# Hybrid decoder layer: negated attention scores, mLSTM keys scaled on ScalarE, one product of the gate spread on VectorE, and bias copies placed later in the program

## The chip, the cores and the metric

One NeuronCore of a Trainium2 chip runs the whole layer in one launch. The engines are TensorE (PE, with its weight loads PEld), VectorE (DVE), ScalarE (ACT), GpSimd (POOL) and SyncE (SP, which issues most transfers). The metric is the device time of one execution in microseconds (us), the median of several runs.

## The reference, cut to what matters

A layer maps x (1024 tokens, 1024 channels) to x of the same shape. It normalises x, projects it, runs an mLSTM (4 heads of 128) and a windowed attention (8 heads of 64) side by side, projects their outputs back, and then retrieves experts.

```python
h = rms_norm(x, norm1_g); proj = h @ w_in
# mLSTM: chunks of 128, with a state carried from chunk to chunk
c = silu(causal_short_conv(u, conv_w, conv_b))
qm = c @ wq_m;  km = (c @ wk_m) * 128 ** -0.5
c_chunk = einsum('bhnl,bhnlk,bhnlv->bhnkv', exp(g - m_loc), km, vm)
# attention: scores with a position bias, softmax by the running maximum
s = einsum(q, k) * 64 ** -0.5 + bias
p = exp(s - max(s)); o = p @ v / sum(p)
x = x + concat(ym, ya) @ w_out
# PEER: 8 heads, top 16 of 128 x 128 experts, per token 128 experts
idx, gate = top_k(...), softmax(...)
a = gelu(x_norm . expert_u[idx]) * gate
x = x + a @ expert_v[idx]
```

## The kernel before

The tokens are eight tiles of 128. They go through the first part in three groups: group 0 is tiles 0 and 1, group 1 is tiles 2 to 5, group 2 is tiles 6 and 7. For each group `channels_in`, `project_gates`, `project_conv`, `project_values` and `project_attention` multiply by the input weights, which `halves` loads in blocks (`wr`) and splits into a rounded part on ACT (`wh`, L168) and a remainder on DVE (`wl`, L170). `attention` and `mlstm` follow, woven together, then `queries`: the output projection (`acco`), the second norm (its GpSimd power is `r2o`), the query projection (`accq`) and the top-16 search on DVE.

The experts are done in two ways. The 512 tokens of group 1 go through all 16,384 experts on PE (`dense_experts`, tiles `pu` and `pv`, 6,144 matmuls of 512 columns), with a matrix of gates that is zero where an expert wasn't chosen. `spread_gates` builds that matrix: for four tokens at a time DVE makes one-hot rows (`hot`, L724), ACT copies one side (`e1`, L728), the other side is multiplied by the gate (`e2`), PE multiplies the two (`pg`, L739) and ACT copies the result out (`gs`, L740). Of the 128 steps of four tokens, every second one has `e2` made by ACT in four instructions (L732), the others by one GpSimd product (L734). In the trace both `e1` and `e2` are called `e`.

The other 512 tokens (tiles 0, 1, 6, 7) are sparse: GpSimd gathers one expert row for 128 tokens at a time by an indirect transfer (`gt`, L803, five buffers). `experts_in` multiplies a gathered row by the token on DVE (L815, `idx`); `experts_out_pe` of tiles 0 and 1 sums the gathered rows by PE (`pov`, L846, with weights `wv` by DVE, `idxt`), `experts_out` of tiles 6 and 7 by DVE (L860). These gathers run beside everything else from the second norm of group 0 on.

The position bias of the attention is made at the start: `rel_d` holds a row of 1152 numbers for each head, and eight transfers copy each row 128 times to `skew_d[h]` in DRAM (L134, 576 KB each), from which `attention_operands` later reads shifted windows (`bt`).

In `scores`, PE makes up to 512 scores at a time (`sc`, L511), DVE adds the bias and keeps the running maximum in one instruction (L513), a small DVE instruction negates the maximum (L516), and ACT takes the exponential with it as bias (L517). In `mlstm`, the keys `pk` are scaled by a factor for each token and by 128 ** -0.5 on DVE (`kt`, L428) and enter the state's update (`pcc`, `cst`). Once a head, GpSimd takes a power there (`sm`, L465).

The program is written in the order of the last lines, but the order in which each engine runs it is set when it is built: `TileContext(nc, schedule_with_timeline_sim=True)` lays the instructions out by a simulated timeline, so an edit anywhere can move instructions elsewhere. Each engine then runs its own list in order, and waits at an instruction whose inputs or buffers aren't ready.

Of the kernel before, what the change touches and what calls it, by code (L numbers as in the profile page):

```python
# [11 lines left out]
F32 = mybir.dt.float32  # L12
# [4 lines left out]
AF = mybir.ActivationFunctionType  # L17
ALU = mybir.AluOpType
# [25 lines left out]
def hybrid_layer(ctx, tc, x, g1, w_in, w_if, conv_w, conv_b, wq, wk, if_b, mh_g, skip, qn_g, kn_g,  # L44
# [84 lines left out]
        nc.sync.dma_start(rel_d, rv)  # L129

    skew_d = {}
    for h in range(AH):
        skew_d[h] = dram.tile([P, RL], F32, name=f"skew{h}")
        nc.sync.dma_start(skew_d[h], rel_d[h:h + 1].to_broadcast([P, RL]))  # L134


    halo = consts.tile([P, MH, 3], F32, name="halo")
# [216 lines left out]
    def gates(g, cl, ml, gi, gf):  # L354

        tile0, n = GROUPS[g]
        full = [MH, n, P]
        mr = cl.tile(full, F32, name="mr", bufs=2)
        ab = ml.tile([MH, n * P], F32, name="ab", tag="w2r", bufs=2)
        nc.vector.scalar_tensor_tensor(ab, gf, -1.0, gf, op0=ALU.mult, op1=ALU.max)  # L360
        nc.scalar.activation(ab, ab, AF.Exp, scale=-1.0)
        nc.scalar.activation(ab, ab, AF.Ln, bias=1.0)
        nc.vector.scalar_tensor_tensor(gf, gf, 0.0, ab, op0=ALU.min, op1=ALU.subtract)
        bc = ml.tile(full, F32, name="bc")
        for c in range(n):
            f = gf[:, c * P:(c + 1) * P]
            nc.vector.tensor_tensor_scan(bc[:, c], f, f, 0.0, op0=ALU.add, op1=ALU.bypass)
        nc.vector.tensor_tensor(gi, gi, bc, op=ALU.subtract)

        top = ml.tile([MH, n], F32, name="top")  # L370
        nc.vector.tensor_reduce(top, gi, AX.X, ALU.max)
        nc.vector.tensor_tensor_scan(mst[:, tile0 + 1:tile0 + n + 1], top, bc[:, :, P - 1],
                                     mst[:, tile0:tile0 + 1], op0=ALU.max, op1=ALU.add)
        for c in range(n):
            t = tile0 + c
            nc.vector.tensor_tensor_scan(mr[:, c], gi[:, c], gi[:, c], mst[:, t:t + 1], op0=ALU.max, op1=ALU.max)
        pc = pst.tile([P, 4, n, MH], F32, name="pc", tag="tp")
        for q in range(4):
            row = gi
            if q:  # L380
                row = ml.tile(full, F32, name="row", tag="w2r", bufs=2)
            if q == 1:
                nc.vector.tensor_tensor(row, mst[:, tile0:tile0 + n, None].to_broadcast(full), mr,
                                        op=ALU.subtract)
            elif q == 2:
                nc.vector.scalar_tensor_tensor(row, bc, -1.0, mr, op0=ALU.mult, op1=ALU.subtract)
            elif q == 3:
                nc.vector.tensor_tensor(row, gi, mr[:, :, P - 1:P].to_broadcast(full), op=ALU.subtract)
            for c in range(n):
                nc.tensor.transpose(pc[:, q, c], row[:, c], ident[0:MH, 0:MH])  # L390
        wcol = cl.tile([P, n, MH], F32, name="wcol", bufs=2)
        nc.vector.tensor_copy(wcol, pc[:, 0])
        ecol = cl.tile([P, 3, n, MH], F32, name="ecol", bufs=2)
        nc.scalar.activation(ecol, pc[:, 1:4], AF.Exp)
        pa = pst.tile([P, n, MH], F32, name="pa", tag="tp")
        nc.tensor.matmul(pa, lastsel, ecol[:, 0], start=True, stop=True)
        acol = cl.tile([P, n, MH], F32, name="acol", bufs=2)
        nc.vector.tensor_copy(acol, pa)
        return mr, wcol, ecol, acol

    def mlstm(g, half, h, ml, cols, mix):
# [23 lines left out]
            nc.tensor.matmul(pk[:, c], cT[:, c * P:(c + 1) * P], wqk[:, 1], start=True, stop=True)  # L425
        kt = ml.tile([P, HT, P], F32, name="kt", tag="w2m", bufs=5 if g == 0 else 6)
        for c in range(HT):
            nc.vector.tensor_scalar(kt[:, c], pk[:, c], ecol[:, 2, c, h:h + 1], P ** -0.5,  # L428
                                    op0=ALU.mult, op1=ALU.mult)
        pd = pml.tile([P, HT, P], F32, name="pd", tag="ml")  # L430
        nc.tensor.matmul(pd, negsel[:, h], mr, start=True, stop=False)
        nc.tensor.matmul(pd, ident, mask[:, None, :].to_broadcast([P, HT, P]), start=False, stop=True)
# [67 lines left out]
    def scores(g, at, op, hp, i):  # L500
        kp, vp, qp, bts, po, den = op
        hs = slice(hp * AD, (hp + 1) * AD)
        NP = (GROUPS[g][0] + GROUPS[g][1]) * P
        W = (GROUPS[g][0] + i + 1) * P
        mx = at.tile([P, 4], F32, name="mx", bufs=4)
        ss = at.tile([P, NP], F32, name="ss", bufs=2)
        m = LOW
        for u0 in range(0, W, 512):
            u1 = min(W, u0 + 512)
            sc = psc.tile([P, 512], F32, name="sc")  # L510
            nc.tensor.matmul(sc[:, :u1 - u0], qp[hs, i * P:(i + 1) * P], kp[hs, u0:u1], start=True, stop=True)  # L511
            j = 1 if u1 == W else 0
            nc.vector.tensor_tensor_reduce(ss[:, u0:u1], sc[:, :u1 - u0], bts[hp][:, NP - W + u0:NP - W + u1],  # L513
                                           1.0, m, ALU.add, ALU.max, mx[:, j:j + 1])
            m = mx[:, j:j + 1]
        nc.vector.tensor_scalar(mx[:, 2:3], mx[:, 1:2], -1.0, None, op0=ALU.mult)  # L516
        nc.scalar.activation(ss[:, :W], ss[:, :W], AF.Exp, bias=mx[:, 2:3], accum_out=den[:, hp, i:i + 1])  # L517
        return ss

    def values(g, at, op, hp, i, ss):  # L520
# [191 lines left out]
    def spread_gates(t, gb, psg):  # L712

        half = TQ
        for b in range(P // TB):
            gs = gb.tile([P, P, TB], F32, name="gs", bufs=2)
            for q in range(TB // half):
                c0 = b * TB + q * half
                ids, gate = ROWS[t]
                full = [P, P, half]  # L720
                hot = []
                for side in range(2):
                    o = gb.tile(full, BF16, name="hot", bufs=6)
                    nc.vector.tensor_tensor(o, ids[:, side, None, c0:c0 + half].to_broadcast(full),  # L724
                                            key128, op=ALU.is_equal)
                    hot.append(o.rearrange("p e t -> p t e"))
                e1 = gb.tile([P, half, P], F32, name="e1", bufs=3)
                nc.scalar.copy(e1, hot[0])  # L728
                e2 = gb.tile([P, half, P], F32, name="e2", bufs=3)
                if q % 2:  # L730
                    for j in range(half):
                        nc.scalar.activation(e2[:, j], hot[1][:, j], AF.Copy, scale=gate[:, c0 + j:c0 + j + 1])  # L732
                else:
                    nc.gpsimd.tensor_tensor(e2, hot[1], gate[:, c0:c0 + half, None].to_broadcast([P, half, P]),  # L734
                                            op=ALU.mult)
                for j0 in range(0, half, 4):
                    pg = psg.tile([P, 4, P], F32, name="pg")
                    for j in range(4):
                        nc.tensor.matmul(pg[:, j], e1[:, j0 + j], e2[:, j0 + j], start=True, stop=True)  # L739
                    nc.scalar.copy(gs[:, :, q * half + j0:q * half + j0 + 4].rearrange("p e t -> p t e"), pg)  # L740
# [139 lines left out]
    cols = project_gates(0, cm.tiles, *hx)  # L880
    project_conv(0, *hx)
    project_values(0, *hx)
    project_attention(0, *hx)
    mx = Scope("mx", "right")
    mix = zq.tiles.tile([P, KD, GROUPS[0][1] * P], F32, name="mix0", tag="z")
# [144 lines left out]
```

## Time and profile before

| what | value |
|---|---|
| runs | 3044.32 us median of 3 (3024.34 to 3048.78) |
| profiled execution | 3025.4 us, its span 3023.6 us |
| mean granted TensorE clock | 0.943 |
| busy share of the span | PE 90%, DVE 78%, POOL 47%, ACT 41% |

The span is the time from the first to the last instruction of one profiled execution. A share of busy time is a mean over stages with different limits: the dense experts fill PE for the second half of the span, while the first half changes its limit several times. The granted clock is that of TensorE, 1.0 for 2.4 GHz and 0.5 for 1.2 GHz.

### The profile page before, as it was taken

What the parts mean: (1) busy time and instruction counts of PE and PEld (TensorE: products, weight loads), DVE (VectorE), ACT (ScalarE), POOL (GpSimd) and SP (SyncE); (2) the same over time, 40 slices, a digit from 0 to 9 for tenths busy, and PEclk for the clock granted to TensorE, in tenths of its full rate; (3) what the DMA queues carried; (4) which work ended last, traced back from release to release, by engine and by line L of the source; (5) the groups of instructions that cost most, each with busy time, mean ns of one, the idle gap of its engine ahead of it and who ended that gap; (6) DMA issues with size and microseconds to landing.
All of it is one profiled execution on the core that took longest, in us unless ns stands there. A gap on an engine that the chain in (4) does not pass through costs nothing.

```text
span 3023.6 us, 42958 instructions
## 1 busy us (share of the span) xinstructions
PE 2735.5 (90%) x14382; PEld 2157.6 (71%) x14382; DVE 2350.9 (78%) x5552; ACT 1231.9 (41%) x2279; POOL 1414.7 (47%) x1139
## 2 busy tenths in 40 slices
PE   6977776898879998888899999999999999999999
PEld 5867665676656664667666787787887877788877
DVE  4559987788976887769854788888888888898873
ACT  4643332364424224899962232233322232232222
POOL 0100567546644445545543555555555555555530
PEclk9979888797889998899999999999999999999999
DMA  6644799898988987898888999999999999999982
GB/s 194 192 153 127 260 322 345 281 326 302 329 310 316 316 306 251 312 327 307 296 299 299 321 332 321 323 333 318 336 331 325 332 324 326 333 335 331 340 287 74
DMA packets 370898, 891.51 MB, mean 295 GB/s; under 512 B 34119, under 2 KB 135495, under 8 KB 366580
## 3 DMA queue, kind: packets, MB, share of 16 engines
q0 software_dynamic: 147456, 536.94, 50.0%
q1 hardware_dynamic: 209076, 307.78, 31.0%
q10 hardware_dynamic: 14144, 44.05, 3.8%
q8 instruction: 113, 1.85, 0.2%
q14 instruction: 109, 0.89, 0.1%
HBM read 831.97 MB, written 61.38 MB: 295 GB/s over the span
## 4 chain that ended last, share of the span: by engine, by line
PE 48%; DMA 13%; issue 13%; DVE 12%; POOL 7%; ACT 6%; SPq 1%; POOLq 0%; DVEq 0%; ACTq 0%
POOL gt L803 7%; DMA gg<-gate_d 5%; PE pu L155 5%; PE pu L154 4%; PE pu L153 4%; PE pv L154 4%; PE pv L153 4%; PE pv L155 4%; PE accq L192 4%; PE pov L846 3%; PE acco L192 3%; DMA gt<-in_expert_u_dram,idx 2%; DVE gt L815 2%; DMA wr<-in_w_in_dram 2%; DMA gt<-in_expert_v_dram,idxt 2%
## 5 line engine op out<-in xcount | busy, mean ns | idle before, releaser
L803 POOL DMA_INDIRECT gt<-in_expert_u_dram,idx x512 | 665.2, 1299 | 630.9 <-DVE gt L815 400.1
L815 DVE SCALAR_TENSOR_TENSOR gt<-gt,h2s 128x1024 f32<-128x1024 f32 x512 | 617.6, 1219 | 71.3 <-DMA gt<-in_expert_u_dram,idx 69.5
L803 POOL DMA_INDIRECT gt<-in_expert_v_dram,idx x256 | 342.5, 1338 | 299.6 <-DVE acc L860 258.5
L154 PE MATMUL pv<-vlo,dah 128*128 128x512 f32 x1024 | 404.1, 395 | 15.1 <-DVE vlo L792 15.0
L803 POOL DMA_INDIRECT gt<-in_expert_v_dram,idxt x256 | 273.3, 1068 | 308.1 <-PE pov L846 250.7
L153 PE MATMUL pu<-h2th,uhi 128*128 128x512 f32 x1024 | 407.3, 398 | 2.2 <-ACT da L765 1.2
L155 PE MATMUL pu<-h2th,ulo 128*128 128x512 f32 x1024 | 407.1, 398 | 1.3 <-DVE ulo L760 1.3
L154 PE MATMUL pu<-h2tl,uhi 128*128 128x512 f32 x1024 | 406.8, 397 | 0.0
L155 PE MATMUL pv<-vhi,dal 128*128 128x512 f32 x1024 | 402.1, 393 | 0.0
L790 ACT CAST vhi<-vr 128x512 fp32r<-128x512 f32 x256 | 158.1, 621 | 457.3 <-PE pv L155 443.8
L860 DVE SCALAR_TENSOR_TENSOR acc<-gt,act,acc 128x1024 f32<-128x1024 f32 x256 | 327.8, 1280 | 10.9 <-DMA gt<-in_expert_v_dram,idx 8.5
L153 PE MATMUL pv<-vhi,dah 128*128 128x512 f32 x1024 | 324.1, 395 | 9.8 <-ACT vhi L790 9.8
L168 ACT CAST wh<-wr 128x512 fp32r<-128x512 f32 x291 | 179.2, 620 | 260.4 <-DMA wr<-in_w_in_dram 55.2
L170 DVE TENSOR_TENSOR wl<-wr,wh 128x512 fp32r<-128x512 f32 x291 | 199.7, 688 | 59.2 <-ACT wh L168 57.3
L792 DVE TENSOR_TENSOR vlo<-vr,vhi 128x512 fp32r<-128x512 f32 x256 | 175.3, 686 | 85.9 <-ACT vhi L790 85.8
L758 ACT CAST uhi<-ur 128x1024 fp32r<-128x1024 f32 x128 | 134.5, 1051 | 262.2 <-PE pu L154 261.8
L154 PEld LDWEIGHTS pv<-vlo,dah 128*128 128x128 f32 x1024 | 193.9, 189 | 64.4 <-DVE vlo L792 20.6
L153 PEld LDWEIGHTS pv<-vhi,dah 128*128 128x128 f32 x1024 | 192.6, 189 | 60.9 <-ACT vhi L790 14.3
L155 PEld LDWEIGHTS pu<-h2th,ulo 128*128 128x128 f32 x1024 | 193.6, 189 | 50.9 <-issue 3.4
L153 PEld LDWEIGHTS pu<-h2th,uhi 128*128 128x128 f32 x1024 | 193.5, 189 | 49.0 <-ACT uhi L758 1.9
L154 PEld LDWEIGHTS pu<-h2tl,uhi 128*128 128x128 f32 x1024 | 193.5, 189 | 47.5 <-issue 1.7
L155 PEld LDWEIGHTS pv<-vhi,dal 128*128 128x128 f32 x1024 | 194.3, 190 | 43.1 <-issue 0.8
(278 smaller groups left out, 5681.9 us busy)
## 6 DMA issues: line engine op xcount, KB each, us to landing
ur<-in_expert_ut_dram SPq DMA_DIRECT2D x128, 512.0 KB, 6.2
vr<-in_expert_v_dram SPq DMA_DIRECT2D x256, 256.0 KB, 5.9
wr<-in_w_in_dram SPq DMA_DIRECT2D x144, 256.0 KB, 5.7
gate_d<-gs ACTq DMA_DIRECT2D x32, 1024.0 KB, 6.6
gg<-gate_d SPq DMA_DIRECT2D x16, 2048.0 KB, 19.4
wr<-in_w_query_dram SPq DMA_DIRECT2D x96, 256.0 KB, 3.9
wr<-in_w_out_dram SPq DMA_DIRECT2D x48, 256.0 KB, 5.0
gt<-in_expert_u_dram,idx POOLq DMA_INDIRECT x512, 7.1
```

What stands on the lines that cost most here:

```text
L153: nc.tensor.matmul(ps, lh, rh, start=first, stop=False)
L154: nc.tensor.matmul(ps, lh, rl, start=False, stop=False)
L155: nc.tensor.matmul(ps, ll, rh, start=False, stop=last)
L168: nc.scalar.copy(wh, wr)
L170: nc.vector.tensor_tensor(wl, wr, wh.bitcast(F32), op=ALU.subtract)
L192: nc.tensor.matmul(o, l, r, start=k == 0 and c == 0 and j == 0, stop=k == KD - 1 and j == 2, skip_group_check=True)
L758: nc.scalar.copy(uh, ur)
L790: nc.scalar.copy(vh, vr)
L792: nc.vector.tensor_tensor(vl, vr, vh.bitcast(F32), op=ALU.subtract)
L803: nc.gpsimd.indirect_dma_start(out=gt, out_offset=None, in_=table, in_offset=bass.IndirectOffsetOnAxis(ap=idx[:, j:j + 1], axis=0))
L815: nc.vector.scalar_tensor_tensor(gt, gt, 1.0, h2, op0=ALU.mult, op1=ALU.mult, accum_out=pr[:, j:j + 1])
L860: nc.vector.scalar_tensor_tensor(acc, gt, COEF[t][:, j:j + 1], acc, op0=ALU.mult, op1=ALU.add)
```

## The change

Four edits. The scores are kept negated: the one DVE instruction now forms -(score + bias) and a running minimum, and the exponential takes its input times -1, so that the small negation L516 goes. The keys' second factor 128 ** -0.5 is multiplied once into a column of `ecol` for each group, and the scaling of the keys becomes an ACT instruction. The GpSimd product of the spread becomes the same product on DVE. And the code that issues the bias copies stands behind the first `project_values`.

```diff
-    for h in range(AH):
-        skew_d[h] = dram.tile([P, RL], F32, name=f"skew{h}")
-        nc.sync.dma_start(skew_d[h], rel_d[h:h + 1].to_broadcast([P, RL]))
+    def skew(heads):
+        for h in heads:
+            skew_d[h] = dram.tile([P, RL], F32, name=f"skew{h}")
+            nc.sync.dma_start(skew_d[h], rel_d[h:h + 1].to_broadcast([P, RL]))
...
+        nc.vector.tensor_scalar(ecol[:, 2], ecol[:, 2], P ** -0.5, None, op0=ALU.mult)
...
-            nc.vector.tensor_scalar(kt[:, c], pk[:, c], ecol[:, 2, c, h:h + 1], P ** -0.5,
-                                    op0=ALU.mult, op1=ALU.mult)
+            nc.scalar.activation(kt[:, c], pk[:, c], AF.Copy, scale=ecol[:, 2, c, h:h + 1])
...
-        m = LOW
+        m = -LOW
...
-                                           1.0, m, ALU.add, ALU.max, mx[:, j:j + 1])
+                                           -1.0, m, ALU.add, ALU.min, mx[:, j:j + 1])
...
-        nc.vector.tensor_scalar(mx[:, 2:3], mx[:, 1:2], -1.0, None, op0=ALU.mult)
-        nc.scalar.activation(ss[:, :W], ss[:, :W], AF.Exp, bias=mx[:, 2:3], accum_out=den[:, hp, i:i + 1])
+        nc.scalar.activation(ss[:, :W], ss[:, :W], AF.Exp, scale=-1.0, bias=mx[:, 1:2],
+                             accum_out=den[:, hp, i:i + 1])
...
-                    nc.gpsimd.tensor_tensor(e2, hot[1], gate[:, c0:c0 + half, None].to_broadcast([P, half, P]),
+                    nc.vector.tensor_tensor(e2, hot[1], gate[:, c0:c0 + half, None].to_broadcast([P, half, P]),
...
     project_values(0, *hx)
+    skew(range(AH))
     project_attention(0, *hx)
```

By count, DVE loses 64 negations and 32 key scalings and gains 64 products and 3 small scalings; ACT gains 32 key scalings; POOL loses 64 products; PE and SP keep the number of their instructions.

**The bias copies.** SP's list at the start of the program, before (`wr` are weight blocks, `skew` the copies):

```order
L166 DMA wr<-in_w_in_dram 128x512
L129 DMA rel_d<-rv 8x1152
L166 DMA wr<-in_w_in_dram 128x512
L134 DMA skew_145<-rel_d 128x1152
L134 DMA skew_147<-rel_d 128x1152
L134 DMA skew_149<-rel_d 128x1152
L134 DMA skew_151<-rel_d 128x1152
L134 DMA skew_153<-rel_d 128x1152
L134 DMA skew_155<-rel_d 128x1152
L134 DMA skew_157<-rel_d 128x1152
L134 DMA skew_159<-rel_d 128x1152
L166 DMA wr<-in_w_in_dram 128x512
```

and now, up to the first read of a bias:

```order
L129 DMA rel_d<-rv 8x1152
L168 DMA wr<-in_w_in_dram 128x512
L136 DMA skew_824<-rel_d 128x1152
L168 DMA wr<-in_w_in_dram 128x512
L136 DMA skew_826<-rel_d 128x1152
L136 DMA skew_828<-rel_d 128x1152
L136 DMA skew_830<-rel_d 128x1152
L136 DMA skew_832<-rel_d 128x1152
L136 DMA skew_834<-rel_d 128x1152
L136 DMA skew_836<-rel_d 128x1152
L136 DMA skew_838<-rel_d 128x1152
L495 DMA bt<-skew_824 128x256
```

One weight block has moved from behind the eighth copy to behind the first; the copies themselves stay where they were, and the rows that follow (three reads of a bias, ten weight blocks) are the same in both.

**The gathers.** POOL's list at the end of group 1's attention, up to the norm behind its output projection (`sm` is the power of one mLSTM head, `r2o` that of the norm, `rqo` those of group 2's attention projections), before:

```order
L161 TENSOR_TENSOR rqo<-rq,mhalf 128x8
L803 DMA gt<-in_expert_u_dram,idx 128x1024 x7
L161 TENSOR_TENSOR rqo<-rq,mhalf 128x8
L465 TENSOR_TENSOR sm<-sm,mhalf 128x2
L803 DMA gt<-in_expert_u_dram,idx 128x1024 x7
L161 TENSOR_TENSOR rqo<-rq,mhalf 128x8
L803 DMA gt<-in_expert_u_dram,idx 128x1024 x11
L465 TENSOR_TENSOR sm<-sm,mhalf 128x2
L803 DMA gt<-in_expert_u_dram,idx 128x1024 x14
L465 TENSOR_TENSOR sm<-sm,mhalf 128x2
L803 DMA gt<-in_expert_u_dram,idx 128x1024 x29
L161 TENSOR_TENSOR r2o<-r_8378,mhalf 128x4
```

and now:

```order
L467 TENSOR_TENSOR sm<-sm,mhalf 128x2
L806 DMA gt<-in_expert_u_dram,idx 128x1024 x4
L163 TENSOR_TENSOR rqo<-rq,mhalf 128x8
L806 DMA gt<-in_expert_u_dram,idx 128x1024 x12
L467 TENSOR_TENSOR sm<-sm,mhalf 128x2
L806 DMA gt<-in_expert_u_dram,idx 128x1024 x10
L467 TENSOR_TENSOR sm<-sm,mhalf 128x2
L806 DMA gt<-in_expert_u_dram,idx 128x1024 x31
L163 TENSOR_TENSOR r2o<-r_8333,mhalf 128x4
L806 DMA gt<-in_expert_u_dram,idx 128x1024 x2
L467 TENSOR_TENSOR sm<-sm,mhalf 128x2
L806 DMA gt<-in_expert_u_dram,idx 128x1024 x7
```

Before, all 256 gathers of `experts_in` for tiles 0 and 1 stood ahead of `r2o`; now 9 of them stand behind it. Counted over POOL's whole list from group 1's first `sm` to `r2o`, 145 gathers stood there before and 130 now, and 111 and 117 stood ahead of that first `sm`. On PE, 16 more of the 512 `pov` matmuls stand behind the last `pg` (84 for 68).

**The spread.** DVE's list in the first half of `spread_gates` (`x` is the output projection's sum of group 2), before:

```order
L724 TENSOR_TENSOR hot<-ids,key_107 128x512 x8
L838 SCALAR_TENSOR_TENSOR wv<-iota_103,aT 128x64
L724 TENSOR_TENSOR hot<-ids,key_107 128x512 x4
L838 SCALAR_TENSOR_TENSOR wv<-iota_103,aT 128x64
L724 TENSOR_TENSOR hot<-ids,key_107 128x512
L569 TENSOR_TENSOR x_13012<-x_13012,acco 128x256 x2
L724 TENSOR_TENSOR hot<-ids,key_107 128x512
L569 TENSOR_TENSOR x_13014<-x_13014,acco 128x256
```

and now:

```order
L727 TENSOR_TENSOR hot<-ids,key_107 128x512 x2
L572 TENSOR_TENSOR x_12951<-x_12951,acco 128x256 x2
L572 TENSOR_TENSOR x_12953<-x_12953,acco 128x256 x2
L737 TENSOR_TENSOR e_11231<-hot,grow 128x512
L727 TENSOR_TENSOR hot<-ids,key_107 128x512 x4
L172 TENSOR_TENSOR wl<-wr,wh 128x512
L841 SCALAR_TENSOR_TENSOR wv<-iota_103,aT 128x64
L727 TENSOR_TENSOR hot<-ids,key_107 128x512 x2
L737 TENSOR_TENSOR e_11264<-hot,grow 128x512
```

The products stand between the one-hot rows, one for every four of them, and whatever stands behind a product on DVE waits with it. Of the 64, 26 stand ahead of the first top-16 search of group 2, 37 between it and the last `hot`, and one behind that.

## Rows read from the trace of the kernel before

**Rows 1.** Windows by stage: busy us (instructions), granted clock, DMA share, GB/s.

```profile
core 0: us, PE busy (x) PEld busy (x) DVE busy (x) ACT busy (x) POOL busy (x), PEclk, DMA share, GB/s
535.00:922.00 387.00, 331.71 (x1932) 263.10 (x1930) 318.39 (x752) 173.56 (x396) 217.73 (x170) 0.85 0.89 311
922.00:1203.00 281.00, 269.02 (x1501) 160.58 (x1501) 218.10 (x1200) 95.93 (x181) 131.72 (x129) 0.95 0.85 295
1203.00:1360.00 157.00, 129.39 (x933) 98.00 (x929) 107.94 (x270) 138.59 (x285) 88.68 (x80) 0.90 0.89 315
1360.00:1541.00 181.00, 155.84 (x1141) 122.76 (x1142) 165.76 (x636) 170.03 (x328) 91.96 (x84) 0.96 0.84 297
1600.00:3010.00 1410.00, 1384.99 (x5983) 1110.91 (x5982) 1131.63 (x1517) 407.01 (x612) 705.87 (x533) 0.99 0.90 313
```

**Rows 2.** Chain of waits, shares by line, 535 to 922 us.

```profile
by line: PE acco L192 12.2%; DVE gt L815 12.1%; DMA gt<-in_expert_u_dram,idx 9.9%; issue 9.6%; DMA wr<-in_w_in_dram 6.9%; PE sc L511 6.2%; PE po L532 4.6%; DVE wl L170 3.0%; POOL gt L803 2.9%; PE pp L528 2.5%; DMA wr<-in_w_out_dram 2.1%; DM
```

**Rows 3.** Timeline of the start: start us, us, engine, line, what.

```profile
18.86 5.57 SPq L134 DMA_DIRECT2D skew<-rel_d  x8
...
24.53 0.59 SPq L166 DMA_DIRECT2D wr<-in_w_in_dram  x1
...
32.57 23.64 SPq L166 DMA_DIRECT2D wr<-in_w_in_dram  x10
...
39.44 0.62 ACT L168 CAST wh<-wr 128x512 fp32r<-128x512 f32 x1 [5.97 <-DMA wr<-in_w_in_dram]
...
40.11 0.58 PE L192 MATMUL accu<-hth,wh 128*128 128x256 f32 x1 [4.75 <-ACT wh L168]
...
42.01 1.12 ACT L168 CAST wh<-wr 128x512 fp32r<-128x512 f32 x2
```

**Rows 4.** Lines L516, L428 and L448: count, ns min/median/max, first and last start.

```profile
L516 DVE TENSOR_SCALAR mx<-mx x64: 134/146/155, 133.1 to 1185.0; 128x1 f32<-128x1 f32 x64
...
L428 DVE TENSOR_SCALAR kt<-pk,ecol x32: 329/342/351, 67.9 to 1150.7; 128x128 f32<-128x128 f32 x32
...
L448 ACT ACTIVATE it<-pn,ecol x32: 349/370/376, 80.3 to 1180.2; 128x129 f32<-128x129 f32 x32
```

**Rows 5.** Tile gt, 535 to 922 us.

```profile
L815 DVE SCALAR_TENSOR_TENSOR gt<-gt,h2s x157: 1173/1217/1280, 534.4 to 921.3; 128x1024 f32<-128x1024 f32 x157
L815 DVE DVE_READ_ACCUMULATOR gt<-gt,h2s x156: 70/81/86, 535.5 to 914.0; 128x1 f32 x156
```

**Rows 6.** Waits, 1150 to 1600 us: total us, times, longest.

```profile
POOL e L734 <- PE pg L739: 35.8, 10, 9.9
...
ACT gs L740 <- PE pg L739: 21.9, 16, 5.1
...
DVE hot L724 <- POOL e L734: 16.1, 8, 3.2
```

**Rows 7.** Tile hot, 1203 to 1558 us, and groups by line, 1190 to 1560 us.

```profile
L724 DVE TENSOR_TENSOR hot<-ids,key x255: 368/414/1946, 1202.7 to 1541.8; 128x512 bf16<-128x512 bf16 x128
...
L734 POOL TENSOR_TENSOR e<-hot,grow x64: 1039/1058/1893, 1209.2 to 1544.5; 128x512 f32<-128x512 bf16 x64
...
L724 DVE TENSOR_TENSOR hot<-ids,key 128x512 bf16<-128x512 bf16 x256 | 125.5, 509 | 51.0 <-ACT e L728 26.4 <-POOL e L734 16.1 <-ACT e L732 7.2
```

**Rows 8.** The page's group of `wl`: busy us, mean ns, idle before.

```profile
L170 DVE TENSOR_TENSOR wl<-wr,wh 128x512 fp32r<-128x512 f32 x291 | 199.7, 688 | 59.2 <-ACT wh L168 57.3
```

**Rows 9.** Timeline in the spread: a product and the `hot` beside it, and one alone.

```profile
1403.81 2.27 POOL L734 TENSOR_TENSOR e<-hot,grow 128x512 f32<-128x512 bf16 x2
1404.02 1.16 DVE L724 TENSOR_TENSOR hot<-ids,key 128x512 bf16<-128x512 bf16 x1
...
1406.92 0.41 DVE L724 TENSOR_TENSOR hot<-ids,key 128x512 bf16<-128x512 bf16 x1
```

**Rows 10.** Chain in the spread: a piece of `pov`. Tile gt from 1560 us: the last gathers.

```profile
1223.34 1.07 PE pov L846 x8
...
L803 POOL DMA_INDIRECT gt<-in_expert_v_dram,idx x256: 939/1152/2288, 1972.8 to 2926.7; - x128
```

More of the change, by code (lines that the diff above doesn't have):

```diff
@@ L504, in scores @@
         W = (GROUPS[g][0] + i + 1) * P
-        mx = at.tile([P, 4], F32, name="mx", bufs=4)
+        mx = at.tile([P, 2], F32, name="mx", bufs=4)
         ss = at.tile([P, NP], F32, name="ss", bufs=2)
-        m = LOW
+        m = -LOW
         for u0 in range(0, W, 512):
```

## The prediction, made before the changed kernel ran

> **What bounds the kernel now.** I read the busy time by stage first, then the chain of waits inside the stages that the change touches, then the waits and the single instructions there. The windows [rows 1] show two halves. From 1600 to 3010 us PE is busy 1385 of 1410 us at a granted clock of 0.99: this stretch is the dense experts, none of the four edits is in it, and its PE work is the same number of matmuls after the change. The sparse gathers that run beside it start their last one at 2926.7 us [rows 10], about 97 us before the end, so a few gathers more in that half cost nothing. The time therefore changes by what the first 1560 us gain or lose.
>
> There the limit moves. From 535 to 922 us (group 1's attention and output projection) PE is busy 332 of 387 us at a clock of 0.85, and DVE 318 [rows 1]. The chain there [rows 2] passes PE, the DVE product of a gathered row (L815) and the gather itself in turn: a loop of gather and product shares DVE's in-order list with the layer's main work. From 922 to 1203 us PE is busy 269 of 281 us and is the limit. In the spread ACT is the limit: 138.6 of 157 us in the first half and 170.0 of 181 in the second, where DVE has 165.8, which is 92% [rows 1].
>
> **The start (bias copies).** By the order, one weight block overtakes seven of the eight copies and nothing else moves; the change hardly does what its words say. In the trace this block is issued at 24.53 us behind the copies and its cast on ACT starts at 39.44 us; PE waits 4.75 us for it [rows 3]. With one copy ahead it lands in time. But the next block is issued at 32.57 us, still behind all copies, and its cast starts at 42.01 [rows 3]. PE gains at most the 4.75 us; it may wait the same at the next block (0). I take -2, the middle.
>
> **The small instructions.** On DVE 64 negations of 0.146 us and 32 key scalings of 0.342 us go, 9.3 and 10.9 us [rows 4]; the three scalings of `ecol` cost about one negation each, 0.4 us. ACT gains 32 instructions; the nearest row is L448, the same form from PSUM with one column more, 0.370 us [rows 4], together 11.8 us. Three quarters of both lie in groups 0 and 1 and a quarter in group 2, and ACT is under half busy in 535 to 1203 us [rows 1], so that these hide behind its waits. Queued behind a key scaling on ACT are exponentials and weight casts, and the state's update waits for the key itself: if that cover were gone, the full 11.8 us would be lost. The gain has the bounds 0 and 20 us. The negations stand between DVE's maximum and ACT's exponential, but PE has other woven work meanwhile. I take -4, a fifth, since what is removed from DVE pays only where DVE is the one waited for.
>
> **The gathers that move.** This is a side effect of the new order, on POOL and DVE: 9 of the gathers that stood ahead of group 1's `r2o` now stand behind it. Each takes 1.217 + 0.081 us of DVE for its product and the read of its sum [rows 5], together 11.7 us. In 535 to 922 us a gather passes every 387 / 157 = 2.46 us [rows 1, 5]; if that loop sets the pace, 9 fewer are worth 22 us. If PE sets it, nothing. I take -12, the DVE time, because DVE is 82% busy there and stands on the chain, but PE with 86% stands on it too. The 9 gathers are next in 922 to 1203 us, where DVE has 63 us free beside a full PE. They push the PE sums of gathered rows back: 16 `pov` matmuls, each two records of the trace, move behind the spread. Eight records take 1.07 us [rows 10], so this is 4.3 us, taken from one stretch in which PE is full and given to another: 0.
>
> **The spread.** The 64 GpSimd products take 1.058 us each [rows 7]. On DVE the nearest row is the 128x512 product of two fp32 tiles with an fp32 result, 0.688 us [rows 8]; I take it, 44 us in all. The bounds are the 0.414 us of the all-bf16 `hot` [rows 7] (26 us) and GpSimd's own 1.058 (68 us). Something comes back: a `hot` beside a running product took 1.16 us, one alone 0.41 [rows 9]; the mean of the 256 is 0.509 against a median of 0.414 [rows 7], so 256 x 0.095 = 24 us of DVE time go with the products. Net DVE gets 20 us, at worst 44.
>
> What the products held up: ACT waited 21.9 us for PE's `pg`, and DVE 16.1 us for a product to free its `hot` buffers [rows 6]. In the first half DVE goes from 107.9 to 107.9 + 26 x 0.688 - 108 x 0.095 = 115.5 of 157 us, ACT stays the limit, and its idle time of 18 us can shrink; I take half, -8 (one more is not worth claiming). In the second half DVE goes to 165.8 + 37 x 0.688 - 148 x 0.095 = 177 of 181 us. There what ACT might gain, DVE takes: 0. The bounds for the spread are ACT's idle time, 18 + 11 = 29 us of gain, and below, in the second half with products at 1.058 and nothing given back, 165.8 + 39 = 205 for 181 us: 24 us of loss.
>
> The SBUF page of the Trainium skill (SBUF — State Buffer, "Who interferes with whom") says more than these rows: a DVE instruction with two SBUF inputs and a GpSimd instruction that reads SBUF shut each other out for the whole instruction. By that rule all 64 x 1.058 = 68 us would come back to DVE instead of 24, and the time would be that of rival 3. The 1.16 us agree with it, the mean of 0.509 doesn't show it for every product.
>
> **The sum.** -2 - 4 - 12 - 8 = -26 us. Against the profiled execution, 3025.4 us, that is 2999. The profiled execution lies 19 us below the median of 3044.32, near the fastest of the three runs; a median of new runs will lie between the two, so I add 10: 3009 us. With all four terms at their better bound the change is -5 - 20 - 22 - 29 = -76; I don't expect them together.
>
> **Rivals.**
> 1. *Hidden anyway.* The stage 535 to 922 us is PE's (86% busy, and slow by its clock of 0.85 rather than by DVE), and the spread stays ACT's with another wait in the place of the product. Only the start and a little of the rest remain, -5: 3020, and 10 for the median, 3030 us. For it speaks ACT's 91% of the spread [rows 1]; against it the gather loop on the chain [rows 2].
> 2. *The gathers set the pace.* 22 us instead of 12, and as the gather loop's waits go, the small instructions count in full on DVE, 20 instead of 4: -52, 2983 us with the 10. For it speaks that the chain names the gather and its product; against it that PE's own share is as large.
> 3. *The lock was the spread's cost.* Every product held up a two-input DVE instruction, and with it ACT. Without products on POOL the second half has 165.8 + 25.5 - 37 x 1.058 = 152 us of DVE work, ACT is the limit throughout, and 29 us of idle time go instead of 8: -47, 2988 us. The rule cited above would make this the case. Against it: two thirds of the products' time left no mark on `hot`.
> 4. *Slower: a waiting product stops DVE.* On POOL a product waited 35.8 us in all for PE's `pg` to free its buffer [rows 6], and nothing but gathers stood behind it. On DVE the one-hot rows, the weight remainders for PE and the top-16 search stand behind it. With those 35.8 us and the 24 us of the worse bound the spread grows by 60; less 14 for the earlier gathers and the start that is +46: 3071, with the 10 3081 us. It decides from the point where DVE's second half passes 181 us, which it misses by 4. Against it: the list puts each product several one-hot rows behind its input, and with three buffers for `e2` a wait should be rarer than on POOL.
>
> **How the numbers follow.** Forecast 0.40 (own range 2996 to 3026), hidden 0.27, gathers 0.11, lock 0.13, slower 0.09. About 1% (30 us) is what a measurement of this kernel can tell from no change, since its three runs lie 24 us apart. Against the median of 3044.32, 1% faster is 3014: that takes a little over half of the forecast's chance, nearly all of rivals 2 and 3 and a tenth of rival 1, 0.47 together. Slower by over 1% is most of rival 4 alone, 0.07. The rest, 0.46, is within 1%. The range of 8 in 10 is 2972 to 3046: it reaches past rivals 2 and 3 by some 10 us, covers rival 1 with its spread, and leaves out most of rival 4 and what lies beyond two terms at their best bounds.
>
> **What the changed kernel's profile would show.** The start: the cast that started at 39.44 us no longer behind a wait of 6 us, PE's 4.75 us gone or moved one block on. The gathers: `r2o` of group 1 earlier by 10 to 20 us. The spread: `hot` at a mean near 0.41 us, the product on DVE near 0.69, DVE above 95% in the second half, and the time from the first to the last `pg` shorter by some 8 us. The dense half: unchanged in length. I would be wrong if the order puts PE's `pov` ahead of gathers that land late, so that PE waits in the 922 to 1203 us stretch, or if the granted clock falls in other places than before: each tenth of clock over 75 us is worth some 8 us, and this is the main uncertainty that no row bounds.

## The result, and the profile after

| kernel | median | runs | ratio [95%] |
|---|---|---|---|
| before | 3034.99 us | 6 (3020.48 to 3048.78) | 1 |
| changed | 3001.19 us | 6 (2996.83 to 3008.5) | 0.9886 [0.9862, 0.9911] |

The change is worth 1.14%, 33.8 us between the medians. I had forecast 3009 us. The profiled execution of the changed kernel took 3002.0 us, its span 3000.2, at a mean granted clock of 0.948 (before: 3025.4, 3023.6 and 0.943).

The same windows as in [rows 1], of the changed kernel:

```profile
535.00:922.00 387.00, 332.04 (x1937) 265.16 (x1938) 304.90 (x690) 175.61 (x415) 201.33 (x164) 0.85 0.88 308
922.00:1203.00 281.00, 269.79 (x1532) 167.85 (x1531) 236.82 (x1225) 107.93 (x203) 130.57 (x130) 0.95 0.88 302
1203.00:1360.00 157.00, 131.66 (x981) 102.78 (x977) 112.22 (x337) 145.78 (x302) 56.16 (x49) 0.93 0.90 325
1360.00:1541.00 181.00, 155.56 (x1099) 118.05 (x1097) 148.92 (x607) 164.90 (x310) 69.55 (x54) 0.96 0.88 314
1600.00:3010.00 1410.00, 1375.43 (x5962) 1100.12 (x5961) 1127.14 (x1513) 402.21 (x606) 706.73 (x535) 1.00 0.89 313
```

In 535 to 922 us DVE is 13.5 us less busy than before and PE is as busy as it was (332.0 for 331.7 us): DVE's freed time shows no gain of PE's there. In the spread's second half DVE has 148.9 us where I feared 177. In its first half ACT rose from 138.6 to 145.8 us, so its idle time shrank by 7.

The page's totals by engine, first before, then after:

```profile
PE 2735.5 (90%) x14382; PEld 2157.6 (71%) x14382; DVE 2350.9 (78%) x5552; ACT 1231.9 (41%) x2279; POOL 1414.7 (47%) x1139
```

```profile
PE 2728.0 (91%) x14382; PEld 2154.0 (72%) x14382; DVE 2337.4 (78%) x5522; ACT 1237.2 (41%) x2311; POOL 1347.6 (45%) x1075
```

Span less PE's busy time is PE's idle time: 288.1 us before, 272.2 after. Of the span's 23.4 us, 15.9 are idle time of PE and 7.5 are less busy time for the same matmuls, at a higher mean clock. By the windows the idle time falls by 0.3 us in 535 to 922, by 0.8 in 922 to 1203 and by 2.0 in 1203 to 1541 (157 + 181 us less PE's busy time, of the rows above and of [rows 1]). By windows of the same kind the rest is 3.1 us up to 535, 2.3 from 1541 to 1600 and 7.3 in the dense half.

These windows stand still while the stages move. The same columns, cut at the first and the last start of `pg` (ahead of the spread, the spread, behind it), before and then after:

```profile
0.00:1210.30 1210.30, 1005.54 (x6066) 782.23 (x6066) 927.17 (x3105) 494.14 (x1026) 517.20 (x432) 0.89 0.80 271
1210.30:1556.90 346.60, 295.44 (x2108) 228.88 (x2109) 272.93 (x900) 314.68 (x618) 179.28 (x165) 0.93 0.87 309
1556.90:3023.60 1466.70, 1434.56 (x6210) 1146.44 (x6209) 1150.84 (x1547) 423.11 (x636) 718.18 (x543) 0.99 0.89 311
```

```profile
0.00:1203.00 1203.00, 1006.49 (x6077) 791.85 (x6077) 924.25 (x3031) 506.21 (x1066) 494.70 (x423) 0.89 0.79 269
1203.00:1533.00 330.00, 279.22 (x2046) 214.39 (x2043) 260.79 (x941) 308.20 (x608) 124.85 (x103) 0.95 0.89 317
1533.00:3000.20 1467.20, 1442.34 (x6266) 1147.73 (x6265) 1152.37 (x1552) 422.82 (x637) 728.09 (x550) 1.00 0.90 316
```

PE's idle time goes from 204.8 to 196.5 us ahead of the spread, from 51.2 to 50.8 in it and from 32.1 to 24.9 behind it.

The start, timeline of the changed kernel (against [rows 3]):

```profile
19.94 0.54 SPq L168 DMA_DIRECT2D wr<-in_w_in_dram  x1
20.53 4.53 SPq L136 DMA_DIRECT2D skew<-rel_d  x7
...
32.33 23.23 SPq L168 DMA_DIRECT2D wr<-in_w_in_dram  x10
32.84 0.62 ACT L170 CAST wh<-wr 128x512 fp32r<-128x512 f32 x1 [2.11 <-PE pif L156]
...
41.14 1.94 ACT L170 CAST wh<-wr 128x512 fp32r<-128x512 f32 x3 [3.89 <-DMA wr<-in_w_in_dram]
...
41.81 0.58 PE L194 MATMUL accu<-hth,wh 128*128 128x256 f32 x1 [4.58 <-ACT wh L170]
```

The cast that started at 39.44 us starts at 32.84, and PE's wait of 4.75 us is now one of 4.58 us for the next block, which is still issued behind all copies.

The spread: groups by line, 1190 to 1560 us, and the first and last start of `pg`, after (against [rows 7]) and before:

```profile
L727 DVE TENSOR_TENSOR hot<-ids,key 128x512 bf16<-128x512 bf16 x256 | 101.8, 418 | 32.3 <-ACT e L731 25.3 <-ACT e L735 5.8
...
L737 DVE TENSOR_TENSOR e<-hot,grow 128x512 f32<-128x512 bf16 x64 | 43.6, 683 | 12.8 <-PE pg L742 12.6
```

```profile
L742 PE MATMUL pg<-e,e x1024: 271/275/583, 1203.0 to 1533.0; 128*128 128x128 f32 x171
```

```profile
L739 PE MATMUL pg<-e,e x1024: 270/275/583, 1210.3 to 1556.9; 128*128 128x128 f32 x171
```

The mean of `hot` went from 509 to 418 ns, and none stretches any more (its longest is 459 ns, by the tile's row). The product on DVE takes 683 ns, so DVE pays 43.6 us and gets 23.7 back. It gets more back from other instructions with two inputs; two lines from the same view, before and after:

```profile
L627 DVE TENSOR_TENSOR cand<-vals 128x16 f32<-128x16 f32 x64 | 13.7, 241 | 0.0
L838 DVE SCALAR_TENSOR_TENSOR wv<-iota,aT 128x64 f32<-128x64 f32 x56 | 15.4, 279 | 6.5 <-PE pov L846 6.4
```

```profile
L630 DVE TENSOR_TENSOR cand<-vals 128x16 f32<-128x16 f32 x64 | 8.8, 165 | 0.0
L841 DVE SCALAR_TENSOR_TENSOR wv<-iota,aT 128x64 f32<-128x64 f32 x56 | 11.9, 217 | 18.6 <-PE pov L849 18.6
```

The spread lasts 330.0 us instead of 346.6. But of these 16.6 us, 16.2 are busy time of PE and only 0.4 idle time: by the trace's records 73 dense matmuls started ahead of the last `pg` before and 48 do now, and 16 `pov` more stand behind it. The shorter stage is mostly PE work that stands elsewhere or runs at a higher clock (0.95 for 0.93).

Waits of the changed kernel, 1150 to 1600 us: total, times, longest (against [rows 6]):

```profile
ACT gs L743 <- PE pg L742: 13.3, 14, 3.2
...
DVE e L737 <- PE pg L742: 12.6, 13, 3.0
```

ACT's wait for PE fell from 21.9 to 13.3 us. The product's wait for `pg` has moved from POOL to DVE, as rival 4 said, but it shrank from 35.8 us to 12.6.

The power `r2o` of group 1, before and after:

```profile
924.29 1.72 POOL L161 TENSOR_TENSOR r2o<-r,mhalf 128x4 f32<-128x4 f32 x1
```

```profile
920.34 1.21 POOL L163 TENSOR_TENSOR r2o<-r,mhalf 128x4 f32<-128x4 f32 x1
```

It is 4 us earlier, not 10 to 20.

### The profile page after: what moved, and what is told of

It is laid out like the page before. It is cut to its first block, busy times and chain, and to the rows that moved or that the text cites. A ratio compares the mean times of both kernels' runs of the same rounds, so it can differ in the third digit from the quotient of the medians.

```text
span 3000.2 us, 42795 instructions
## 1 busy us (share of the span) xinstructions
PE 2728.0 (91%) x14382; PEld 2154.0 (72%) x14382; DVE 2337.4 (78%) x5522; ACT 1237.2 (41%) x2311; POOL 1347.6 (45%) x1075
## 4 chain that ended last, share of the span: by engine, by line
PE 22%; issue 12%; POOL 8%; DMA 7%; DVE 4%; ACT 4%; POOLq 0%; DVEq 0%; ACTq 0%
POOL gt L806 8%; DMA gg<-gate_d 5%; PE pv L156 3%; PE pv L157 3%; PE pu L156 3%; PE pu L155 3%; PE pu L157 3%; PE pv L155 3%; PE pg L742 2%; ACT gs L743 1%; ACT e L735 1%; PE pov L849 1%; DMA gt<-in_expert_u_dram,idx 1%; DVE acc L863 1%; PE accq L194 1%
## 5 line engine op out<-in xcount | busy, mean ns | idle before, releaser
L806 POOL DMA_INDIRECT gt<-in_expert_v_dram,idxt x256 | 285.9, 1117 | 412.1 <-PE pov L849 359.5
```

What stands on the lines that cost most here:

```text
L806: nc.gpsimd.indirect_dma_start(out=gt, out_offset=None, in_=table, in_offset=bass.IndirectOffsetOnAxis(ap=idx[:, j:j + 1], axis=0))
```

## The experiments

Ratios are to the kernel before, run on the same chip in the same rounds; before had medians of 3034.9, 3037.8, 3036.4 and 3033.5 us in the four sets.

### Each edit alone

The product alone:

```diff
-                    nc.gpsimd.tensor_tensor(e2, hot[1], gate[...].to_broadcast([P, half, P]),
+                    nc.vector.tensor_tensor(e2, hot[1], gate[...].to_broadcast([P, half, P]),
```

> Only the product of the spread goes from GpSimd to VectorE; the order of all engines up to the spread is that of the kernel before. If the spread's gain (last pg 24 us earlier, first pg 7 us earlier) is owed to the product, this kernel gains 14 to 18 us, ratio 0.994 to 0.995, all of it between the first and the last pg. If the gain is owed to the shifted order of the whole program, it gains 0 to 4 us, ratio 0.999 to 1.000.

Measured 3013.57 us, 0.9939 [0.9915, 0.9963]. Its spread lasted 340.5 us in the profile (1211.6 to 1552.1), 6.1 less than before, and what follows it was 5.7 us shorter. So the size was as expected, but not that all of it lies between the first and the last `pg`: PE idles 51.5 us there (51.2 before), 25.5 behind it (32.1) and 199.2 ahead of it (204.8).

The copies alone:

```diff
     project_values(0, *hx)
+    skew(range(AH))
```

> Only the code of the bias copies is moved; the order differs from before in one weight block on SyncE's list. The prediction's step (the wait of 4.75 us is half saved) gives -2 us, ratio 0.9993. The rival, read from the trace after, where the wait stands at the next block: 0 us, ratio 1.000, PE's longest wait for a weight cast at the start still 4 to 5 us.

Measured 3032.32 us, 0.999 [0.9966, 1.0014]: nothing that can be told from zero, as the start's rows above suggest.

The negation alone:

```diff
-                                           1.0, m, ALU.add, ALU.max, mx[:, j:j + 1])
+                                           -1.0, m, ALU.add, ALU.min, mx[:, j:j + 1])
...
-        nc.vector.tensor_scalar(mx[:, 2:3], mx[:, 1:2], -1.0, None, op0=ALU.mult)
```

> Only the 64 small negations go; 4 more gathers stand ahead of group 1's first mLSTM power and 6 fewer between it and the norm behind the output projection. If VectorE's freed time (9 us) pays only in part, it gains 2 to 5 us, ratio 0.998 to 0.9995. If each negation stands on the path between maximum and exponential, 9 us and more, ratio 0.997 or less.

Measured 3035.23 us, 1.0003 [0.9982, 1.0024]. Within the interval of 6 us either way, the 64 instructions that went were hidden.

The keys alone:

```diff
-            nc.vector.tensor_scalar(kt[:, c], pk[:, c], ecol[:, 2, c, h:h + 1], P ** -0.5,
-                                    op0=ALU.mult, op1=ALU.mult)
+            nc.scalar.activation(kt[:, c], pk[:, c], AF.Copy, scale=ecol[:, 2, c, h:h + 1])
```

> Only the key scaling goes from VectorE to ScalarE. The copies and the negation alone gave nothing, so if the 25 us of the kernel with all three edits are the keys' own, this one has them: ratio 0.990 to 0.994, with the stretch before the first pg or the end of the spread shorter. If they come only from the order that the three edits give together, 0.998 to 1.002. The prediction had this edit hidden, 0 to -3 us, ratio 0.999.

Measured 3019.77 us, 0.9948 [0.9922, 0.9974], between the two expectations: a real gain, where my prediction had put nearly nothing.

All edits but the product:

```diff
-                    nc.vector.tensor_tensor(e2, hot[1], gate[...].to_broadcast([P, half, P]),
+                    nc.gpsimd.tensor_tensor(e2, hot[1], gate[...].to_broadcast([P, half, P]),
```

> The copies, the negation and the keys as in the changed kernel, the product left on GpSimd. If the terms add up, it gains what the changed kernel gains less the product: 6 to 9 us, ratio 0.997 to 0.998, and first pg 7 us earlier than before. If the gathers set the pace of group 1 (rival 2 of the prediction), 20 us or more, ratio 0.993 or less.

Measured 3010.04 us, 0.9899 [0.9856, 0.9942]. Six runs from 2980 to 3021 us make this interval wide: it holds the sum of the three edits alone (0.994) at its very end. Alone this would say that the three work better together; the next two runs fit edits that add up. The ratio also lies where I expected it if the gathers set the pace of group 1. But its `r2o` starts at 925.4 us, no earlier than before (924.3), with the nine gathers behind it, so that isn't how this kernel gains.

### Do the two gains add up?

Product and keys, without the negated scores and the later copies (diff against the changed kernel):

```diff
-                                           -1.0, m, ALU.add, ALU.min, mx[:, j:j + 1])
+                                           1.0, m, ALU.add, ALU.max, mx[:, j:j + 1])
...
-    skew(range(AH))
```

> The two edits that gained alone, the product on DVE and the keys on ACT, without the negated scores and the later copies. If gains belong to the edits and add up, this has the whole gain: 0.994 x 0.995 = 0.989, ratio 0.987 to 0.991. If the half per cent of the keys alone belongs to the order that its build happened to get, it needn't come with the product, and the ratio lies at 0.992 to 0.996.

Measured 2996.23 us, 0.9862 [0.9808, 0.9916], four runs. The whole gain is there without the other two edits.

The changed kernel with the keys on DVE again:

```diff
-            nc.scalar.activation(kt[:, c], pk[:, c], AF.Copy, scale=ecol[:, 2, c, h:h + 1])
+            nc.vector.tensor_scalar(kt[:, c], pk[:, c], ecol[:, 2, c, h:h + 1], P ** -0.5,
+                                    op0=ALU.mult, op1=ALU.mult)
```

> The changed kernel with the keys scaled on DVE as before. If gains belong to the edits and add up, half of the gain is left, that of the product: ratio 0.992 to 0.995. If the whole gain needs no keys on ACT (the order of the full change would give it anyway), it stays at 0.987 to 0.990.

Measured 3014.01 us, 0.9928 [0.9903, 0.9952]. It is the product's gain and no more. So the gain of the change is that of two edits, and each has it in company as alone within the intervals, though the builder gives each of these kernels another order.

### What did the GpSimd product cost?

The changed kernel, with an idle GpSimd product beside each product on DVE. It reads a constant and the gates and writes a tile that nobody reads:

```diff
+                    junkp = gb.tile([P, half, P], F32, name="jp2", bufs=1)
+                    nc.gpsimd.tensor_tensor(junkp, key128.rearrange("p e t -> p t e"),
+                                            gate[...].to_broadcast([P, half, P]), op=ALU.mult)
```

> The changed kernel, with a second product of the same shape on GpSimd for each of the 64 that VectorE makes, from a constant and into a tile that nobody reads. If the GpSimd product cost the spread by shutting VectorE's two-input instructions out (rival 3), hot goes back to a mean near 0.5 us, the spread grows by 10 us or more and the ratio to the kernel before is 0.992 to 0.995. If it cost by what waited for its result, the ratio stays at the changed kernel's 0.989, within 0.002, though hot is slower.

Measured 3039.49 us, 0.9997 [0.9972, 1.0023], worse than either expectation: more than the product's own share is lost, the whole gain is gone. Groups by line of this kernel, 1150 to 1600 us:

```profile
L727 DVE TENSOR_TENSOR hot<-ids,key 128x512 bf16<-128x512 bf16 x256 | 132.9, 543 | 15.2 <-ACT e L731 11.6 <-ACT e L735 2.9
...
L740 POOL TENSOR_TENSOR jp<-key,grow 128x512 f32<-128x512 bf16 x64 | 72.4, 1131 | 3.1
...
L737 DVE TENSOR_TENSOR e<-hot,grow 128x512 f32<-128x512 bf16 x64 | 53.9, 843 | 17.9 <-PE pg L745 17.9
```

Nobody waits for these 64 instructions, yet `hot` takes 31 us more and the product on DVE 10. Its timeline (start, us) shows what happens beside one of them:

```profile
1230.39 1.44 DVE L679 TENSOR_TENSOR one<-one 128x256 bf16<-128x256 bf16 x1
1230.63 1.05 POOL L740 TENSOR_TENSOR jp<-key,grow 128x512 f32<-128x512 bf16 x1
...
1232.43 1.82 DVE L691 TENSOR_TENSOR ef<-ef,smx 128x128 f32<-128x128 f32 x1
1233.05 1.05 POOL L740 TENSOR_TENSOR jp<-key,grow 128x512 f32<-128x512 bf16 x1
...
1234.38 0.41 DVE L727 TENSOR_TENSOR hot<-ids,key 128x512 bf16<-128x512 bf16 x1
```

The same `one` and `ef` take 0.24 and 0.28 us in the kernel of the next rows. Both stretched DVE instructions (`one` from 1230.39, `ef` from 1232.43) end 0.15 us after the GpSimd product beside them.

A GpSimd instruction in the same place could also cost by its time ahead of the gathers. So the next kernel has there one that takes about as long (1.2 us) and writes as many elements, of half the size, to a tile nobody reads, but reads nothing:

```diff
+                    junkp = gb.tile([P, P, half], BF16, name="jp2", bufs=1)
+                    nc.gpsimd.iota(junkp, pattern=[[1, P], [0, half]], base=0, channel_multiplier=0,
+                                   allow_small_or_imprecise_dtypes=True)
```

> The changed kernel, with 64 GpSimd instructions in the places of the old products that write a tile nobody reads and read no data from SBUF (1.2 us each by an iota of this size in the traces). If the cost of the GpSimd product was that it read SBUF while two-input DVE instructions did, the gain stays: ratio 0.986 to 0.992, mean of the one-hot rows 0.42 us, spread 325 to 345 us. If the cost was the time on GpSimd's list, ahead of the gathers, the gain goes as with the idle product: ratio 0.997 to 1.002, spread above 360 us, whatever the one-hot rows take.

Measured 2996.99 us, 0.9885 [0.9851, 0.9919]: the gain of the change, unharmed. Groups by line, 1150 to 1600 us, and two rows of the timeline:

```profile
L727 DVE TENSOR_TENSOR hot<-ids,key 128x512 bf16<-128x512 bf16 x256 | 101.6, 417 | 27.1 <-ACT e L731 18.1 <-ACT e L735 5.1 <-issue 2.7
...
L740 POOL IOTA jp<- 128x512 bf16 x64 | 76.7, 1198 | 2.5
L737 DVE TENSOR_TENSOR e<-hot,grow 128x512 f32<-128x512 bf16 x64 | 43.8, 686 | 11.1 <-PE pg L745 9.9 <-issue 0.6 <-DVE hot L727 0.4
```

```profile
1226.80 0.24 DVE L679 TENSOR_TENSOR one<-one 128x256 bf16<-128x256 bf16 x1
...
1227.98 0.28 DVE L691 TENSOR_TENSOR ef<-ef,smx 128x128 f32<-128x128 f32 x1
```

GpSimd is busy for 76.7 us with these, even longer than with the products (72.4), and `hot` stays at 417 ns. So it isn't GpSimd's time that costs. What the product does and this instruction doesn't is read SBUF, the on-chip memory that holds the tiles. (It also writes twice the bytes; this pair of kernels doesn't separate the two.) The first and last start of `pg`, with the idle product and with the instruction that reads nothing:

```profile
L745 PE MATMUL pg<-e,e x1024: 270/275/583, 1203.1 to 1576.5; 128*128 128x128 f32 x171
```

```profile
L745 PE MATMUL pg<-e,e x1024: 271/275/583, 1205.1 to 1538.6; 128*128 128x128 f32 x171
```

373 us against 333: the same program but for that instruction, and 40 us in the spread, 42.5 between the medians. PE idles 66.3 us in the spread for 46.9, and 301.1 for 270.0 in the whole program.

### Is ACT the spread's limit?

The changed kernel with ACT's half of the products on GpSimd:

```diff
-                if q % 2:
-                    for j in range(half):
-                        nc.scalar.activation(e2[:, j], hot[1][:, j], AF.Copy, scale=gate[:, c0 + j:c0 + j + 1])
+                eng = nc.gpsimd if q % 2 else nc.vector
+                eng.tensor_tensor(e2, hot[1], gate[...].to_broadcast([P, half, P]), op=ALU.mult)
```

> The changed kernel, with the other half of the products (four ScalarE instructions each, 85 us in all) on GpSimd; VectorE keeps its 64. If ScalarE is the limit of the spread, the stretch from the first to the last pg shrinks from 330 us to 290 (PE's busy time there), ratio 0.974 to 0.980. If VectorE is as close to its limit as the prediction had it (177 of 181 us in the second half), or the GpSimd products slow it, the spread shrinks by 0 to 10 us, ratio 0.985 to 0.990.

Measured 3034.54 us, 0.9997 [0.9972, 1.0023], outside both expectations. It brought the products that read back to GpSimd, and `hot` is at 508 ns again. That the spread nevertheless shrank to 306 us (1214.0 to 1519.9) made me try it without GpSimd, all 128 products on DVE:

```diff
-                if q % 2:
-                    for j in range(half):
-                        nc.scalar.activation(e2[:, j], hot[1][:, j], AF.Copy, scale=gate[:, c0 + j:c0 + j + 1])
-                else:
-                    nc.vector.tensor_tensor(e2, hot[1], gate[...].to_broadcast([P, half, P]),
+                nc.vector.tensor_tensor(e2, hot[1], gate[...].to_broadcast([P, half, P]),
```

> The changed kernel with the other half of the products, too, on DVE as one instruction each instead of four on ACT: ACT gets 85 us back in the spread, DVE gives 43, and GpSimd reads nothing there. If ACT's time in the spread sets the end, the spread goes from 330 to about 300 us and the ratio to 0.976 to 0.982. If the end is set by what PE has to do in all, so that a shorter spread only moves its work behind the spread, the ratio stays at 0.985 to 0.992.

Measured 3011.15 us, 0.9927 [0.9894, 0.9959], just beyond the second expectation: no faster than the change, and slower by the medians, though the two intervals overlap. The `pg` of this kernel:

```profile
L738 PE MATMUL pg<-e,e x1024: 270/275/583, 1213.3 to 1505.1; 128*128 128x128 f32 x171
```

The spread lasts 292 us, 38 less than with the change, and the time is 10 us longer. By the order no dense matmul stands ahead of the last `pg` any more (48 of them in the changed kernel) and 100 of the `pov` stand behind it (84). Of the 38 us, 24.4 are busy time of PE (254.8 for 279.2) and 13.8 its idle time (37.0 for 50.8). So with less work on ACT, PE does wait less in the spread, but most of the shorter stage is work moved out of it; and behind the last `pg` PE idles 40.2 us instead of 24.9, in the whole program 278.0 instead of 272.2. That ACT alone sets the spread's length isn't shown.

### Where do the keys gain?

The kernel before with the keys on ACT, and the same scaling once more on DVE into a tile nobody reads, so that DVE gets nothing back:

```diff
+            nc.scalar.activation(kt[:, c], pk[:, c], AF.Copy, scale=ecol[:, 2, c, h:h + 1])
+            ktj = ml.tile([P, P], F32, name="ktj")
-            nc.vector.tensor_scalar(kt[:, c], pk[:, c], ecol[:, 2, c, h:h + 1], P ** -0.5,
+            nc.vector.tensor_scalar(ktj, pk[:, c], ecol[:, 2, c, h:h + 1], P ** -0.5,
```

> The kernel before with the keys scaled on ACT, and the same 32 scalings done once more on DVE into a tile nobody reads. If the half per cent of the keys alone came from DVE's freed 11 us or from what follows it in DVE's list, it goes: ratio 0.998 to 1.002. If it came from the key's new place on ACT (earlier keys, another order of PE's dense work behind them), it stays: 0.993 to 0.996.

Measured 3023.66 us, 0.9963 [0.9938, 0.9987]. A gain clear of zero stays without DVE's freed 11 us, so they are not the whole of it; whether they are a part, the intervals of this kernel and of the keys alone leave open. An earlier `r2o` isn't needed either: here it starts at 940.1 us, 16 us later than before. One place differs in the traces. PE's longest waits from 780 to 1000 us (total us, times, longest; `hn` is the normed output of an mLSTM head, `pth` its transpose), before and with the keys alone:

```profile
PE pth L470 <- DVE hn L467: 17.5, 1, 17.5
```

```profile
PE acco L192 <- ACT mixh L554: 5.9, 1, 5.9
...
PE pth L470 <- DVE hn L467: 3.4, 1, 3.4
```

At the end of group 1, PE stands idle for 17.5 us before the last mLSTM head; the attention's last product (`ya`, 825.8 us) runs 18 us ahead of that head's power (`sm`, 844.2). With the keys on ACT it runs 4 us ahead (831.0 and 834.9), so that attention work covers more of the head. With the doubled scaling the wait is 4.5 us, with product and keys 5.0. But the negation alone also cuts it, to 10.2 us, and gains nothing, and the full change has it at 9.7 us with its whole gain. So this wait isn't settled as the keys' gain. The traces can't settle it: the profiled executions of the keys alone (3029.8 us) and of the doubled scaling (3030.5) lie 10 and 7 us above their medians, and above the profiled one of before (3025.4). Where those 16 us come from stays open.

## Why the prediction was right, and where its steps were not

The total came near, a forecast of -26 against 23.4 us between the profiled executions, but by luck: the terms were not right, and their errors cancelled. Nor were the 10 us for the median right: before has its median at 3035, 9.6 us above its profiled execution, but the changed kernel has it 0.8 below its own, so 3009 was 8 us too high. By the runs of the edits alone, the product and the keys are worth some 20 and 16 us, where I had 8 and 4; the copies and the gathers, for which I had 14, show nothing.

**The start (-2).** Nothing. The wait moved one block on, which was the bound of 0; the copies alone gave 0.999 [0.9966, 1.0014].

**The small instructions (-4).** The term was right in mechanism for the negation (hidden as far as the runs tell, 1.0003) and mis-sized for the keys: 0.5% or 16 us alone, and 0.4 to 0.8% in company (no_keys against the change, product alone against product and keys). I had priced the keys and the negation together at a fifth of DVE's freed time; keys_twice keeps 0.4% with none of it freed. That step failed: moving an instruction was costed only by the engines' time, and what else pays here (when the key arrives, or what the builder's order makes of it) isn't shown.

**The gathers that move (-12).** This failed most clearly. `r2o` came 4 us earlier, and PE's idle time in 535 to 922 us fell by 0.3 us. Of the two bounds, 22 us and nothing, the lower is near. In the six kernels with nine gathers behind it, `r2o` starts between 915.6 and 925.4 us, before at 924.3, and with the keys alone, three gathers behind it, at 916.5: their number doesn't set it. What does isn't shown; PE still idles 55 us of the 387. The chain names what was waited for last; it doesn't say that a shorter wait there shortens the rest.

**The spread (-8).** It was mis-sized: the product is worth 0.6 to 0.7% between medians (product alone, no_keys), some 20 us. Nor does it come where I had it. ACT's idle time in the first half shrank by 7 us, nearly the 8 that I took, and the spread is 16.6 us shorter, but PE's idle time in it fell by 0.4 us; it fell by 8.3 ahead of the spread and by 7.2 behind it. Behind the last `pg` PE idles 20 to 30 us in the five kernels with ACT's half of the products and no GpSimd product that reads, and 29 to 44 us in the seven with one; why the gain shows there isn't settled. The price on DVE was right (0.683 for 0.688 us; 101.8 us of `hot` for an expected 101). What I left out is that `hot` was not the only DVE instruction held up: in the kernel before, `cand` and `wv` took 8.4 us more, and idle_product shows `one`, `ef` and the products stretched as well. My second half of 177 us came out at 148.9, 82% and not above 95. The length behind the last `pg` stayed, as I had said: 1467.2 for 1466.7 us.

**The rivals.** Rival 3, the lock, had the mechanism right, with 0.13 of the chance: a product that reads costs 42 us, an instruction that only writes costs nothing. Its 29 us of ACT's idle time were too much (31.9 to 21.8 us in the spread) and its count for the second half, 152 us, nearly right. My argument against it, that two thirds of the products' time left no mark on `hot`, counted the wrong thing: a lock leaves a mark only while a two-input DVE instruction is due, and not only on `hot`. The Trainium skill says this (SBUF — State Buffer, "Who interferes with whom"): a DVE instruction with two SBUF inputs contends with a GpSimd instruction that reads SBUF, and not with one that only writes it. The two idle kernels agree, 543 against 417 ns. Rival 1 (hidden anyway) held for the copies, the negation and, by `r2o` and PE's idle time, the gathers. Rival 2 fell with the gathers. Rival 4 did not come: the product's wait on DVE was 12.6 us, and DVE's second half stayed 32 us below its end.

## What to carry to other kernels

Before you place an elementwise product on GpSimd because it has time, look at what DVE does beside it: here 64 products that nobody waited for cost 42 us of 3000 when they read SBUF, and 64 instructions of the same length that only wrote cost nothing. In a kernel that fills PE, a shorter stage can be work that has moved: look at PE's idle time in the whole program (278.0 us for 272.2 with the spread 38 us shorter), and trust the medians of several runs over the sum of one profile, which for the keys alone shows 287.0 for 288.1 us where the runs show some 16 us of gain. And take edits apart before crediting them: of four, two gave all of the gain that shows.

## What the runs showed of the hardware that I had not expected

A DVE instruction beside a reading GpSimd product can take several times its time: `ef` with 128 elements in each partition took 1.82 us for 0.28, `one` with 256 took 1.44 for 0.24.

The time of one kernel follows its mean granted clock from run to run. In 88 runs of the kernel before, from 3018 to 3057 us, the clock lies between 0.934 and 0.945; the median time is 3039.7 us for the 35 runs from 0.936 to 0.938 and 3026.6 for the 15 at or above 0.942. The changed kernel's runs have 0.943 to 0.949. Whether the clock is higher because PE idles less, or the reverse, these runs don't tell; a difference of single profiles of 10 us is no evidence by itself.
